# Values first in layer 0, rotary tables built a quarter wide, and the first weights on ScalarE's queue

## The chip, the core and the metric

The kernel runs on one core of a Trainium2 chip. The core has TensorE (PE: matmuls, with weight loads, PEld, beside them), VectorE (DVE), ScalarE (ACT), GpSimd (POOL), SyncE (SP, which here issues transfers) and 16 DMA engines that all queues share. The metric is device time in microseconds (us) of one execution.

## The reference, cut to what is computed

Two layers work on x, 256 tokens by 2048 channels, in f32. Each layer does:

```python
h = rms_norm(x, norm_g[l])
proj = einsum('btd,dc->btc', h, w_in[l])          # 6848 columns
rw_in, g_rw, q, k_at, v_at, g_at = split(proj)
r, k, v, xw, xa = split(bidir_token_shift(rw_in, shift_mu[l]))
y_rw = rwkv7_branch(r, k, v, xw, xa, ...)         # 16 heads, one scan per direction
qh, kh = rope(q, positions), rope(k_at, positions)
y_at = window_attention(qh, kh, v_at, sink[l])    # 16 query heads, 4 key heads, |i-j| <= 128
mix = concatenate([y_rw * silu(g_rw), y_at * silu(g_at)])
x = x + einsum('btc,cd->btd', mix, w_out[l])
```

`rope` needs the sine and cosine of position times 32 frequencies. A final rms_norm follows.

## The kernel before

Activations lie channels by tokens. The f32 products are made of a high and a low part: every weight tile of 128 x 1024 is loaded into `raw` (three buffers, SP's queue, `wload`), split by `wsplit` into `hi` (ScalarE, L239) and `lo` (VectorE, L241), two buffers each, and every 128 x 128 block of it takes three matmuls of 256 columns (L309 to L311). Such a triple is called a step here. `Stream` holds the steps of all projections in one order; `S.run(n)` issues the next n of them, and when two steps of a tile are left it issues the load and split of the next one. A layer has 864 input steps (xw and xa 32, eight head pairs of k, v, r and gate 512, attention values 32, keys 32, queries and gates 256) and 256 output steps: 2240 in all.

`window(64, ...)` runs 64 steps in 11 groups and lets generators go on between the groups: `scan_p`, `scan_i` and `scan_b` (preparation, inversion and recurrence of one head pair, one pair behind the other), `attend`, and in layer 0 `setup`, which makes constants and the rotary tables. Lists such as `ROT` and `ATT` say in which groups each goes on. TensorE's order is the program's; the other engines' instructions are placed by a scheduler with priorities, apart from those issued through `PA` and `PV`, which keep the program's order.

At the start SP's queue loads the first weight tile, norm_g, x in five parts and the second tile. ScalarE and VectorE split each of the 16 rows of x (`x_split`, L203 and L204) while TensorE, after 11 warm-up matmuls, runs one step of xw for each row. Then ScalarE squares x for the norm in four parts. Layer 0's attention values (`v_step`, L578 to L580) came in window 8; windows 0 to 9 hold scans, 10 and 11 scans and attention, 12 attention alone. The rotary tables COS and SIN are made in place, 256 tokens wide on all 128 partitions, although only 32 frequencies differ; the range reduction goes on from window 2 to window 6 and the two sine lookups are in window 7.

Of the kernel before, what the change touches and what calls it, by code (L numbers as in the profile page):

```python
# [133 lines left out]
def hybrid_trunk_kernel(ctx, tc, xT, wi, wv, wo, par, fing, dup, iup, sink, pos, cst, out):  # L134
# [207 lines left out]
    COS = cp.tile([128, T], F32, name="COS")  # L342
    SIN = cp.tile([128, T], F32, name="SIN")

    def setup():
        posi = st("t1", [T], I32, bufs=3)
        SY.dma_start(out=posi, in_=pos.to_broadcast([128, T]))
# [4 lines left out]
        for l in range(DEPTH):  # L352
            s = DP[:, l, 0:NSH]
            V.tensor_tensor(s, PR[:, l, P_MU0 : P_MU0 + NSH], PR[:, l, P_MU1 : P_MU1 + NSH], op=ALU.add)
            V.tensor_scalar(s, s, -1.0, 1.0, op0=ALU.mult, op1=ALU.add)
            h = DP[:, l, NSH : NSH + 8]
            V.tensor_scalar(h, PR[:, l, P_KA : P_KA + 8], 0.5, None, op0=ALU.mult)
            V.tensor_scalar(DP[:, l, NSH + 8 : NSH + 16], h, -1.0, 1.0, op0=ALU.mult, op1=ALU.add)
            V.tensor_scalar(DP[:, l, NSH + 16 : NSH + 32], PR[:, l, P_A0 : P_A0 + 16], 0.5, None, op0=ALU.mult)
        V.tensor_scalar(SK, SK, 8.0, None, op0=ALU.mult)  # L360
        yield

        V.tensor_copy(
# [3 lines left out]
        V.memset(MSK, 1.0)  # L367
        V.memset(MSK[:, :, 0:1], 0.0)
        V.tensor_copy(band, cin[:, 0:512])
        A.activation(BONES, ones, AF.Copy, scale=0.0)  # L370
        for r in half:
            A.activation(BONES[r, r], ones[r, r], AF.Copy)
        V.tensor_copy(EYE, cin[:, 512 + 64 * NL : 576 + 64 * NL])
        V.tensor_scalar(NEYE, EYE, -1.0, None, op0=ALU.mult)
        V.tensor_scalar(EYE2, EYE, 2.0, None, op0=ALU.mult)
# [9 lines left out]
        def reduce_by(dst, src, period, bits, shift):  # L385
            PV.tensor_scalar(nn, src, 1.0 / period, shift, op0=ALU.mult, op1=ALU.add)
            yield
            PV.tensor_scalar(nn, nn, MAGIC, MAGIC, op0=ALU.add, op1=ALU.subtract)
            yield
            cur = src  # L390
            for p in split_const(period, bits, 4):
                PV.scalar_tensor_tensor(dst, nn, -p, cur, op0=ALU.mult, op1=ALU.add)
                cur = dst
                yield

        two_pi = 2.0 * np.pi
        yield from reduce_by(ang, ang, two_pi * 4096.0, 7, 0.0)
        for dst, shift, add in ((SIN, 0.0, 0.0), (COS, 0.25, np.pi / 2)):
            yield from reduce_by(dst, ang, two_pi, 11, shift)
# [6 lines left out]
        yield  # L406
        PV.tensor_scalar(SIN, SIN, C[:, C_OFF["sgn"] : C_OFF["sgn"] + 1], None, op0=ALU.mult)
# [31 lines left out]
    def queue_inputs(l):  # L439
# [129 lines left out]
        pvs = []  # L569

        def v_step(kk, b):
            def f(w):
                if not pvs:
                    pvs.extend(ps_main.tile([128, T], F32, tag="m", name="pva") for _ in range(2))
                k = kk % 4
                wh, wl = (x[:, k * 256 : (k + 1) * 256] for x in w)
                tb = slice(b * 128, (b + 1) * 128)
                PE.matmul(pvs[b], L.XH[:, kk, tb], wh, start=(kk == 0), stop=False)  # L578
                PE.matmul(pvs[b], L.XH[:, kk, tb], wl, start=False, stop=False)
                PE.matmul(pvs[b], L.XL[:, kk, tb], wh, start=False, stop=(kk == 15))  # L580

            return f

        def v_evac():
            L.VA = st("VA", [2, 256])
            with tc.high_priority(offset=PRIO_B):
                A.activation(L.VA[:, 0, :], pvs[0], AF.Copy, scale=L.norm.rt[:, 0:1])  # L587
                V.tensor_scalar(L.VA[:, 1, :], pvs[1], L.norm.rt[:, 1:2], None, op0=ALU.mult)

        for qt in range(4):  # L590
            S.add(
                lambda qt=qt: wsplit(wload(wv[l, qt])),
                [v_step(qt * 4 + k, b) for k in range(4) for b in range(2)],
                v_evac if qt == 3 else None,
            )

        def k_place(m):
            def place():
                if m == 0:
                    L.KA = [st("KA", [2, T], F32R), [st(n, [T], F32R) for n in ("kd", "kkr")]]  # L600
                return L.KA[0][:, m, :], L.KA[1][m]

            return place
# [68 lines left out]
    def layer(l):  # L672
# [399 lines left out]
        def scores(j):  # L1072
            m, g = divmod(j, 4)
            t = L.tq[j]
            Sc = t["S"] = st("ge", [2, 2, 264], bufs=2) if j == 2 else st("mv", [2, 2, 264], bufs=3)
# [52 lines left out]
        def attend():  # L1128
# [37 lines left out]
    for k in range(NKT):  # L1166
        x_split(L0.XH, L0.XL, X0[:, k, :], k, 0)
        S.run(1)
# [9 lines left out]
    S.later(20, lambda: L0.norm.add([ACC[:, i * T : (i + 1) * T] for i in range(4)]))  # L1178
    S.later(27, lambda: L0.norm.spread())
    S.run(8)  # L1180
    SY.dma_start(out=C, in_=cst[:, 0:C_KEEP])
    SY.dma_start(out=PR, in_=par.rearrange("l p n -> p l n"))
    setup_ = setup()
    next(setup_)
    S.run(8)
    for l in range(DEPTH):
# [5 lines left out]
        if l + 1 < DEPTH:  # L1192
            S.run(32)
# [88 lines left out]
```

## Time and profile before

| | |
|---|---|
| median of 3 runs | 1171.67 us (1170.61 to 1172.37) |
| the profiled execution, its span | 1171.01 us, 1169.2 us |
| TensorE busy | 1148.4 us, 98% |
| VectorE busy | 905.4 us, 77% |
| ScalarE busy | 785.5 us, 67% |
| GpSimd busy | 21.7 us, 2% |
| moved by DMA | 166.63 MB, mean 143 GB/s |

The first row is what the prediction is held to. The profiled execution is one more run, with its own time; its span goes from the first to the last instruction shown. Busy time of TensorE is modelled, and matmuls overlap: one of 256 columns is shown as 0.28 us long while the next starts 0.12 us after it.

### The profile page before, as it was taken

What the parts mean: (1) busy time and instruction counts of PE and PEld (TensorE: products, weight loads), DVE (VectorE), ACT (ScalarE), POOL (GpSimd) and SP (SyncE); (2) the same over time, 40 slices, a digit from 0 to 9 for tenths busy, and PEclk for the clock granted to TensorE, in tenths of its full rate; (3) what the DMA queues carried; (4) which work ended last, traced back from release to release, by engine and by line L of the source; (5) the groups of instructions that cost most, each with busy time, mean ns of one, the idle gap of its engine ahead of it and who ended that gap; (6) DMA issues with size and microseconds to landing.
All of it is one profiled execution on the core that took longest, in us unless ns stands there. A gap on an engine that the chain in (4) does not pass through costs nothing.

```text
span 1169.2 us, 38101 instructions
## 1 busy us (share of the span) xinstructions
PE 1148.4 (98%) x16151; PEld 1074.6 (92%) x16151; DVE 905.4 (77%) x2012; ACT 785.5 (67%) x1986; POOL 21.7 (2%) x23
## 2 busy tenths in 40 slices
PE   8999999999999999999999999999999999999996
PEld 7988999999899999899999899999999999899996
DVE  7889978888877677766668888888887767786554
ACT  6667876787776666655556677876786666675553
POOL 0000000000000000000000000000000000000000
PEclk9999999999999999999999999999999999999998
DMA  7544334333333433477655443334333343346653
GB/s 261 168 152 134 130 106 127 97 112 113 96 116 124 134 120 121 141 238 234 212 177 176 141 135 116 106 108 131 98 112 111 121 136 122 106 144 191 213 192 127
DMA packets 60554, 166.63 MB, mean 143 GB/s; under 512 B 7744, under 2 KB 22880, under 8 KB 60384
## 3 DMA queue, kind: packets, MB, share of 16 engines
q1 hardware_dynamic: 60384, 164.21, 43.8%
q8 instruction: 126, 2.06, 0.7%
q14 instruction: 44, 0.36, 0.1%
HBM read 157.37 MB, written 4.19 MB: 138 GB/s over the span
## 4 chain that ended last, share of the span: by engine, by line
PE 75%; issue 13%; DVE 5%; ACT 4%; DMA 1%; SPq 0%; POOL 0%; POOLq 0%; DVEq 0%; ACTq 0%
PE pm L309 19%; PE pm L311 16%; PE pm L310 16%; PE pg L831 3%; PE pcc L994 2%; DVE lo L241 2%; PE pcc L1022 2%; PE pd L938 1%; PE py L1006 1%; PE py L979 1%; PE pq L929 1%; PE pcc L1012 1%; ACT hi L239 1%; DMA raw<-wi 1%; PE pza L689 1%
## 5 line engine op out<-in xcount | busy, mean ns | idle before, releaser
L241 DVE TENSOR_TENSOR lo<-raw,hi 128x512 fp32r<-128x512 f32 x560 | 372.0, 687 | 115.2 <-ACT hi L239 109.8
L239 ACT ACTIVATE hi<-raw 128x512 fp32r<-128x512 f32 x560 | 329.5, 625 | 169.7 <-PE pm L310 98.0
L309 PE MATMUL pm<-XHa,hi 128*128 128x256 f32 x832 | 245.6, 295 | 0.8 <-ACT VA L587 0.4
L309 PE MATMUL pm<-XHb,hi 128*128 128x256 f32 x832 | 243.5, 293 | 0.2
L311 PE MATMUL pm<-XHb,lo 128*128 128x256 f32 x832 | 234.2, 281 | 1.4 <-DVE lo L241 1.4
L311 PE MATMUL pm<-XHa,lo 128*128 128x256 f32 x832 | 234.1, 281 | 1.2 <-DVE lo L241 1.0
L310 PE MATMUL pm<-XLb,hi 128*128 128x256 f32 x832 | 234.0, 281 | 0.4 <-DVE XLb L204 0.4
L310 PE MATMUL pm<-XLa,hi 128*128 128x256 f32 x832 | 234.2, 281 | 0.1
L309 PEld LDWEIGHTS pm<-XHa,hi 128*128 128x128 f32 x832 | 157.1, 189 | 11.4 <-ACT XHa L203 1.3
L309 PEld LDWEIGHTS pm<-XHb,hi 128*128 128x128 f32 x832 | 157.0, 189 | 6.0 <-ACT hi L239 0.3
L311 PEld LDWEIGHTS pm<-XHa,lo 128*128 128x128 f32 x832 | 157.2, 189 | 2.5 <-DVE lo L241 2.4
L311 PEld LDWEIGHTS pm<-XHb,lo 128*128 128x128 f32 x832 | 157.2, 189 | 2.1 <-DVE lo L241 2.0
L310 PEld LDWEIGHTS pm<-XLa,hi 128*128 128x128 f32 x832 | 157.4, 189 | 0.7 <-DVE XLa L204 0.7
L310 PEld LDWEIGHTS pm<-XLb,hi 128*128 128x128 f32 x832 | 157.3, 189 | 0.6 <-DVE XLb L204 0.6
L1017 ACT ACTIVATE suv<-pcc 64x128 f32<-64x128 f32 x128 | 34.5, 270 | 72.3 <-PE pcc L1015 48.4
L309 PE MATMUL pm<-MHa,hi 128*128 128x256 f32 x256 | 72.0, 281 | 0.0
L311 PE MATMUL pm<-MHb,lo 128*128 128x256 f32 x256 | 71.8, 280 | 0.0
L310 PE MATMUL pm<-MLa,hi 128*128 128x256 f32 x256 | 71.8, 280 | 0.0
L310 PE MATMUL pm<-MLb,hi 128*128 128x256 f32 x256 | 71.7, 280 | 0.0
L309 PE MATMUL pm<-MHb,hi 128*128 128x256 f32 x256 | 71.7, 280 | 0.0
L311 PE MATMUL pm<-MHa,lo 128*128 128x256 f32 x256 | 71.7, 280 | 0.0
L309 PEld LDWEIGHTS pm<-MHa,hi 128*128 128x128 f32 x256 | 48.2, 188 | 0.8 <-issue 0.8
(291 smaller groups left out, 2322.7 us busy)
## 6 DMA issues: line engine op xcount, KB each, us to landing
raw<-wi SPq DMA_DIRECT2D x207, 512.0 KB
raw<-wo SPq DMA_DIRECT2D x64, 512.0 KB
raw<-wv SPq DMA_DIRECT2D x8, 512.0 KB
rrot<-u SPq DMA_DIRECT2D x80, 32.0 KB
vg<-xT SPq DMA_DIRECT2D x16, 128.0 KB
xd<-vg SPq DMA_DIRECT2D x16, 128.0 KB
vg<-xd SPq DMA_DIRECT2D x16, 128.0 KB
g<-dup SPq DMA_DIRECT2D x16, 97.0 KB
```

The source lines that it names most:

```text
L239: A.activation(hi[:, q], raw[:, q], AF.Copy)
L241: V.tensor_tensor(lo[:, q], raw[:, q], hi[:, q].bitcast(F32), op=ALU.subtract)
L309: PE.matmul(pm, wh, rh[:, kk, :], start=(kk == 0), stop=False)
L310: PE.matmul(pm, wh, rl[:, kk, :], start=False, stop=False)
L311: PE.matmul(pm, wl, rh[:, kk, :], start=False, stop=(kk == 15))
L689: PE.matmul(o, w[0], x[0], start=True, stop=False)
L831: PE.matmul(pg[:, h, c * 128 : (c + 1) * 128], BK[half[h], d, c, 1 - h : 3 - h, :].rearrange("p s j -> p (s j)"), MV[half[h], d, c].rearra ...
L929: PE.matmul(narrow(pq[:, d], h ^ d, c), hq(AB, d, c, h), sub(TC, h, d, c, d * b), start=True, stop=True)
L938: PE.matmul(narrow(pd[:, d], h, c), hx(TT, d, c, h), sub(QF, h ^ d, d, c, d * b), start=True, stop=True)
L994: PE.matmul(pc[half[h], 0, d, :], GE[h][r, d, ci[d], 0, :], SUV[r, d, ci[d], h, :], start=True, stop=True)
L1017: A.activation(here(h), pc[half[h], 1], AF.Copy)
L1022: PE.matmul(pS[half[h], d, :], BT[:, h, d, i, :], SUV[:, d, ci[d], h, :], start=(i == 0), stop=True, skip_group_check=True)
```

## The change

Layer 0 now runs its 32 value steps first: each row of x serves two steps (one for each half of the tokens) instead of one, and 32 steps are run while x is split. xw and xa follow, in the two banks of one pair. The windows begin after 64 steps instead of 32. Layer 1 runs its values right after xw and xa, and S.run(64) stands between the layers. Window 12 has 32 steps; the attention begins one window earlier, relative to the scans, and its calls are spread by a new `ATT`. The setup is issued in program order (`PV`, `PA`), spread by a new `ROT` over windows 0 to 4. The rotary angles are laid out as 4 quarters of 64 tokens on 4 groups of 32 partitions, so that each operation is 64 columns wide; sixteen transfers on SP's queue spread the result. The first weights and norm_g are issued by ScalarE. The transfers of C and PR are issued within the loop over x.

```diff
 ATT = [
-    [3, 9],
-    [1, 3, 5, 6, 8, 10],
-    [0, 2, 4, 5, 6, 8, 9, 10],
+    [9],
+    [1, 4, 8],
+    [0, 2, 3, 5, 6, 8, 9],
+    [0, 1, 2, 3, 4],
 ]
-ROT = {0: [2, 3], 1: [], 7: [2, 5, 7], 8: [1, 3], 9: []}
+ROT = ([2, 4, 6, 9], [2, 7], [0, 3, 5, 8], [2, 6], [5])
...
-    first_w = [wrp.tile([128, 1024], F32, tag="raw", name="raw") for _ in range(2)]
+    first_w = [wrp.tile([128, 1024], F32, tag="raw", name="raw") for _ in range(3)]
...
-    SY.dma_start(out=first_w[0][:, 0:512], in_=wi[0, 0, 0, :, 0:512])
-    SY.dma_start(out=G0, in_=par[0, :, P_NG : P_NG + NKT])
+    A.dma_start(out=first_w[0][:, 0:512], in_=wv[0, 0, :, 0:512])
+    A.dma_start(out=G0, in_=par[0, :, P_NG : P_NG + NKT])
     for a, b in ((0, 2), (2, 4), (4, 8), (8, 12), (12, 16)):
         SY.dma_start(out=X0[:, a:b, :], in_=xT[:, a:b, :])
         if a == 0:
-            SY.dma_start(out=first_w[0][:, 512:1024], in_=wi[0, 0, 0, :, 512:1024])
-        if a == 4:
-            SY.dma_start(out=first_w[1], in_=wi[0, 0, 1])
+            SY.dma_start(out=first_w[0][:, 512:1024], in_=wv[0, 0, :, 512:1024])
+        if a in (2, 4):
+            SY.dma_start(out=first_w[a // 2], in_=wv[0, a // 2])
...
-    COS = cp.tile([128, T], F32, name="COS")
-    SIN = cp.tile([128, T], F32, name="SIN")
+    TRIG = cp.tile([128, 2, T], F32, name="TRIG")
+    SIN, COS = TRIG[:, 0], TRIG[:, 1]
     def setup():
-        posi = st("t1", [T], I32, bufs=3)
-        SY.dma_start(out=posi, in_=pos.to_broadcast([128, T]))
+        posi = st("t1", [64], I32, bufs=3)
+        quarter = [slice(i * 32, (i + 1) * 32) for i in range(4)]
+        for i, q in enumerate(quarter):
+            SY.dma_start(out=posi[q], in_=pos[:, i * 64 : (i + 1) * 64].to_broadcast([32, 64]))
...
-        AN = st("VA", [2, T])
-        ang, nn = AN[:, 0], AN[:, 1]
-        V.tensor_copy(ang, posi)
-        yield
+        AN = st("KA", [4, 64])
+        ang, nn, table = AN[:, 0], AN[:, 1], AN[:, 2:4]
+        PV.tensor_copy(ang, posi)
...
-        for dst in (SIN, COS):
-            PA.activation(dst, dst, AF.Sin)
+        PA.activation(table, table, AF.Sin)
         yield
+        PV.tensor_copy(band, cin[:, 0:512])
+        yield
+        for i, q in enumerate(quarter):
+            for r in quarter:
+                SY.dma_start(out=TRIG[r, :, i * 64 : (i + 1) * 64], in_=table[q])
+            yield
         PV.tensor_scalar(SIN, SIN, C[:, C_OFF["sgn"] : C_OFF["sgn"] + 1], None, op0=ALU.mult)
...
+        turns = [(k, b) for k in range(4) for b in range(2)] if l == 0 else [(k, b) for b in range(2) for k in range(4)]
+        done = (lambda: S.later(23, v_evac)) if l == 0 else v_evac
...
         if l == 0:
-            inproj(0, lambda pm: S.later(29, lambda: xw_evac(pm)), raws=first_w, bank=lambda: wbank("pm")[:, 0:T])
-            inproj(1, lambda pm: S.later(13, lambda: xa_evac(pm)))
+            values_in()
...
+        if l == 0:
+            inproj(0, lambda pm: S.later(13, lambda: xw_evac(pm)), bank=lead_bank(0))
+            inproj(1, lambda pm: S.later(4, lambda: xa_evac(pm)), bank=lead_bank(1))
         else:
             inproj(0, xw_evac)
             inproj(1, xa_evac)
+            values_in()
...
-                if j < 6:
+                if 0 < j < 6:
                     scores(j + 2)
                 yield
                 if j < 7:
                     flip(j + 1)
+                    if j == 0:
+                        scores(2)
                     yield
-        for w in range(NP + 2):
-            window(64, *scans(w), *([(setup_, ROT.get(w, [2, 5, 9, 9]))] if l == 0 else []))
+        for w in range(NP + 1):
+            window(64, *scans(w), *([(setup_, ROT[w])] if l == 0 and w < len(ROT) else []))
         att = attend()
-        window(64, *scans(NP + 2), (att, ATT[0]))
-        window(64, *scans(NP + 3), (att, ATT[1]))
-        window(64, (att, ATT[2]))
+        for i in range(3):
+            window(64, *scans(NP + 1 + i), (att, ATT[i]))
+        window(32, (att, ATT[3]), groups=len(ATT[3]))
...
         x_split(L0.XH, L0.XL, X0[:, k, :], k, 0)
-        S.run(1)
+        S.run(2)
+        if k == 11:
+            SY.dma_start(out=C, in_=cst[:, 0:C_KEEP])
+            SY.dma_start(out=PR, in_=par.rearrange("l p n -> p l n"))
...
-    S.later(20, lambda: L0.norm.add([ACC[:, i * T : (i + 1) * T] for i in range(4)]))
-    S.later(27, lambda: L0.norm.spread())
+    S.later(18, lambda: L0.norm.add([ACC[:, i * T : (i + 1) * T] for i in range(4)]))
+    S.later(25, lambda: L0.norm.spread())
+    setup_ = setup()
     S.run(8)
-    SY.dma_start(out=C, in_=cst[:, 0:C_KEEP])
-    SY.dma_start(out=PR, in_=par.rearrange("l p n -> p l n"))
-    setup_ = setup()
     next(setup_)
-    S.run(8)
+    S.run(24)
...
         if l + 1 < DEPTH:
-            S.run(32)
+            S.run(64)
```

## Rows read from the trace of the kernel before

**Rows 1.** The page's busy times: engine, us (share of the span), instructions.

```profile
PE 1148.4 (98%) x16151; PEld 1074.6 (92%) x16151; DVE 905.4 (77%) x2012; ACT 785.5 (67%) x1986; POOL 21.7 (2%) x23
```

**Rows 2.** Timeline of the start: start, us, what, idle before it and its releaser.

```profile
1.22 4.88 PE L1162 MATMUL warm<-QF 128*128 128x512 f16 x11 [1.22 <-DVE QF L1157]
...
1.64 0.43 SPq L325 DMA_DIRECT2D X0a<-xT  x1
...
5.95 0.51 ACT L203 ACTIVATE XHa<-X0a,G 128x256 fp32r<-128x256 f32 x1 [2.00 <-DMA X0a<-xT]
...
6.51 0.58 PE L309 MATMUL pm<-XHa,hi 128*128 128x256 f32 x1 [0.42 <-ACT XHa L203]
...
9.63 0.41 PE L309 MATMUL pm<-XHa,hi 128*128 128x256 f32 x1
...
10.27 0.41 PE L309 MATMUL pm<-XHa,hi 128*128 128x256 f32 x1
...
11.16 0.28 PE L309 MATMUL pm<-XHa,hi 128*128 128x256 f32 x1
...
11.48 3.29 ACT L203 ACTIVATE XHb<-X0b,G 128x256 fp32r<-128x256 f32 x8
11.51 0.28 PE L309 MATMUL pm<-XHa,hi 128*128 128x256 f32 x1
...
15.72 1.99 ACT L254 ACTIVATE mv<-X0a 128x1024 f32<-128x1024 f32 x2
```

**Rows 3.** TensorE's groups by line from 6.40 to 37.15 us: count, busy, mean, idle before.

```profile
L309 PE MATMUL pm<-XHa,hi 128*128 128x256 f32 x32 | 10.1, 314 | 0.4 <-ACT XHa L203 0.4
...
L311 PE MATMUL pm<-XHb,lo 128*128 128x256 f32 x32 | 9.1, 284 | 1.2 <-DVE lo L241 1.2
L216 PE MATMUL pr<-C,mv 128*128 128x1 f32 x16 | 1.8, 245 | 0.0
L224 PE MATMUL pr<-C,rt 128*128 128x128 f32 x4 | 0.6, 274 | 0.0
```

**Rows 4.** The page's costliest groups: the splits of the weights.

```profile
L241 DVE TENSOR_TENSOR lo<-raw,hi 128x512 fp32r<-128x512 f32 x560 | 372.0, 687 | 115.2 <-ACT hi L239 109.8
L239 ACT ACTIVATE hi<-raw 128x512 fp32r<-128x512 f32 x560 | 329.5, 625 | 169.7 <-PE pm L310 98.0
```

**Rows 5.** Windows: span, busy of PE, PEld, DVE, ACT, POOL; granted clock; DMA.

```profile
50.20:78.92 28.72, 27.23 (x242) 26.15 (x240) 26.70 (x51) 20.27 (x45) 0.00 (x0) 1.00 0.50 160
...
189.69:230.53 40.84, 40.29 (x753) 37.25 (x751) 34.97 (x76) 30.52 (x82) 1.31 (x1) 1.00 0.36 110
270.63:313.92 43.29, 41.48 (x753) 38.47 (x751) 35.52 (x75) 33.91 (x86) 1.31 (x1) 0.96 0.33 104
...
764.03:803.89 39.86, 39.86 (x753) 37.03 (x751) 34.01 (x72) 30.41 (x82) 1.31 (x1) 1.00 0.34 113
843.86:883.72 39.86, 39.86 (x753) 37.02 (x751) 34.69 (x74) 30.40 (x82) 1.31 (x1) 1.00 0.36 113
```

**Rows 6.** Timelines of ScalarE and of TensorE near 293 us, in window 7.

```profile
292.80 1.28 ACT L254 ACT_TABLE_LOAD   x1
...
295.54 0.30 PE L938 MATMUL pd<-QF,tt 64*64 64x32 f16 x16 [1.81 <-ACT tt L900]
```

**Rows 7.** The stretch after that wait, columns as in Rows 5.

```profile
297.40:300.80 3.40, 3.40 (x28) 3.18 (x31) 3.13 (x9) 2.88 (x9) 0.00 (x0) 0.50 0.00 0
```

**Rows 8.** The tile VA, VectorE: operations of the range reduction, min/median/max ns.

```profile
L254 DVE SCALAR_TENSOR_TENSOR VA<-VA x4: 416/416/416, 108.1 to 142.9; 128x256 f32<-128x256 f32 x4
```

**Rows 9.** Waits of TensorE and of SP's queue: us in total, times, longest.

```profile
PE pbn L704 <- DVE ip L254: 2.2, 2, 1.1
...
SPq L552 <- ACT u L550: 14.0, 4, 5.4
```

**Rows 10.** Timeline of window 12: last scores, end of their softmax.

```profile
481.26 0.39 PE L1085 MATMUL pscr<-KA,kr 64*128 64x256 f32 x2
...
486.92 0.61 DVE L1103 TENSOR_SCALAR mv<-mv,den 128x256 f32<-128x256 f32 x2
```

More of the change, by code (lines that the diff above doesn't have):

```diff
@@ L353, in setup @@
             s = DP[:, l, 0:NSH]
-            V.tensor_tensor(s, PR[:, l, P_MU0 : P_MU0 + NSH], PR[:, l, P_MU1 : P_MU1 + NSH], op=ALU.add)
-            V.tensor_scalar(s, s, -1.0, 1.0, op0=ALU.mult, op1=ALU.add)
+            PV.tensor_tensor(s, PR[:, l, P_MU0 : P_MU0 + NSH], PR[:, l, P_MU1 : P_MU1 + NSH], op=ALU.add)
+            PV.tensor_scalar(s, s, -1.0, 1.0, op0=ALU.mult, op1=ALU.add)
             h = DP[:, l, NSH : NSH + 8]
[L357 to L360, printed above, removed]
-        yield
-        V.tensor_copy(
+            PV.tensor_scalar(h, PR[:, l, P_KA : P_KA + 8], 0.5, None, op0=ALU.mult)
+            PV.tensor_scalar(DP[:, l, NSH + 8 : NSH + 16], h, -1.0, 1.0, op0=ALU.mult, op1=ALU.add)
+            PV.tensor_scalar(DP[:, l, NSH + 16 : NSH + 32], PR[:, l, P_A0 : P_A0 + 16], 0.5, None, op0=ALU.mult)
+        PV.tensor_scalar(SK, SK, 8.0, None, op0=ALU.mult)
+        V.memset(MSK, 1.0)
+        V.memset(MSK[:, :, 0:1], 0.0)
+        yield
+        PA.activation(BONES, ones, AF.Copy, scale=0.0)
+        for r in half:
+            PA.activation(BONES[r, r], ones[r, r], AF.Copy)
+        PV.tensor_copy(EYE, cin[:, 512 + 64 * NL : 576 + 64 * NL])
+        PV.tensor_scalar(NEYE, EYE, -1.0, None, op0=ALU.mult)
+        PV.tensor_scalar(EYE2, EYE, 2.0, None, op0=ALU.mult)
+        yield
+        PV.tensor_copy(
             LV.rearrange("p l s (n x) -> p (l s) n x", x=32),
@@ L393, in reduce_by @@
                 cur = dst
-                yield
         two_pi = 2.0 * np.pi
-        yield from reduce_by(ang, ang, two_pi * 4096.0, 7, 0.0)
-        for dst, shift, add in ((SIN, 0.0, 0.0), (COS, 0.25, np.pi / 2)):
-            yield from reduce_by(dst, ang, two_pi, 11, shift)
+        reduce_by(ang, ang, two_pi * 4096.0, 7, 0.0)
+        yield
+        for i, (shift, add) in enumerate(((0.0, 0.0), (0.25, np.pi / 2))):
+            dst = table[:, i]
+            reduce_by(dst, ang, two_pi, 11, shift)
             if add:
@@ L494, in split, with v_step, f, v_evac @@
             V.tensor_tensor(lo, x[0:rows], hi.bitcast(F32), op=ALU.subtract)
-        if l == 0:
-            inproj(0, lambda pm: S.later(29, lambda: xw_evac(pm)), raws=first_w, bank=lambda: wbank("pm")[:, 0:T])
-            inproj(1, lambda pm: S.later(13, lambda: xa_evac(pm)))
+        pvs = []
+        def v_step(kk, b):
+            def f(w):
+                if not pvs:
+                    pvs.extend(ps_main.tile([128, T], F32, tag="m", name="pva") for _ in range(2))
+                k = kk % 4
+                wh, wl = (x[:, k * 256 : (k + 1) * 256] for x in w)
+                tb = slice(b * 128, (b + 1) * 128)
+                PE.matmul(pvs[b], L.XH[:, kk, tb], wh, start=(kk == 0), stop=False)
+                PE.matmul(pvs[b], L.XH[:, kk, tb], wl, start=False, stop=False)
+                PE.matmul(pvs[b], L.XL[:, kk, tb], wh, start=False, stop=(kk == 15))
+            return f
+        def v_evac():
+            L.VA = st("VA", [2, 256])
+            with tc.high_priority(offset=PRIO_B):
+                A.activation(L.VA[:, 0, :], pvs[0], AF.Copy, scale=L.norm.rt[:, 0:1])
+                V.tensor_scalar(L.VA[:, 1, :], pvs[1], L.norm.rt[:, 1:2], None, op0=ALU.mult)
+        turns = [(k, b) for k in range(4) for b in range(2)] if l == 0 else [(k, b) for b in range(2) for k in range(4)]
+        done = (lambda: S.later(23, v_evac)) if l == 0 else v_evac
+        raws = first_w if l == 0 else []
+        def values_in():
+            for qt in range(4):
+                S.add(
+                    lambda qt=qt: wsplit(raws[qt] if qt < len(raws) else wload(wv[l, qt])),
+                    [v_step(qt * 4 + k, b) for k, b in turns],
+                    done if qt == 3 else None,
+                )
+        if l == 0:
+            values_in()
+        lead = []
+        def lead_bank(i):
+            def bank():
+                if not lead:
+                    lead.append(wpair("pm"))
+                return lead[0][:, i, 0:T]
+            return bank
+        if l == 0:
+            inproj(0, lambda pm: S.later(13, lambda: xw_evac(pm)), bank=lead_bank(0))
+            inproj(1, lambda pm: S.later(4, lambda: xa_evac(pm)), bank=lead_bank(1))
         else:
@@ L567, in rope_evac @@
             return evac
[L569 to L595, printed above, removed]
         def k_place(m):
```

18 lines of the change are left out of this document (5 added, 13 removed).

## Prediction

> **What bounds the kernel now.** I read the busy times first: TensorE is busy for 98% of the span [rows 1], and its order is the program's. The change keeps every matmul, so it can only take out time in which TensorE waits or runs slowly. The second view is therefore the start. TensorE's first useful matmul comes at 6.51 us, 0.42 us after the warm-up and released by the first split row of x [rows 2]. Up to 37.15 us it makes 64 steps, 32 in each half of the rows, and the norm's 20 small matmuls [rows 3]. At full pace a step takes 0.35 us (11.16 to 11.51), early on 0.64 us (9.63 to 10.27) [rows 2]; 256 columns in 0.21 us are the lower of the two clock levels, 1.2 GHz, and that pace lasted to about 10.6 us. So the floor is 64 x 0.35 + 1.8 + 0.6 = 24.8 us [rows 2, 3], the elapsed time 37.15 - 6.51 = 30.6 us, and 5.8 us are lost: to the low clock, to rows of x that ScalarE and VectorE hand over one by one, and 1.2 us to a late low part of a weight tile [rows 3], after the squares of x had held ScalarE (1.99 us for two of four) [rows 2].
>
> The third view compares the windows of the two layers, which run the same instructions but for the setup in layer 0. The stretches shown are windows 1, 5 and 7 of layer 0 and windows 5 and 7 of layer 1 [rows 5]. Window 5 takes 40.84 us against 39.86, window 7 takes 43.29 against 39.86. In window 7 the chain is plain: ScalarE switches its table for the sines, 1.28 us, and TensorE waits 1.81 us for a small inversion tile tt that stands behind it [rows 6]; then the granted clock is 0.50, the lower level, for 3.4 us, with 28 matmuls in it [rows 7].
>
> **The start.** Values first gives two steps for each split row of x. The warm-up ends at 1.22 + 4.88 = 6.10 us [rows 2]. x now is first on SP's queue, where it stood behind two issues and was issued at 1.64, so the split row should be there by then; 6.51 - 6.10 = 0.4 us come from this. The two issues on ScalarE's queue cost it 2 x 0.43 us, by SP's row, ahead of its first table load, long before it needs x at 5.95 [rows 2]: nothing. If the cover failed, the 0.4 us would be lost again and no more. I keep the low clock to 10.6 us: 4.5 us make 7.0 steps instead of 12.9, so 5.9 x 0.35 = 2.1 us are lost. The squares still come between two weight tiles, so I keep that 1.2 us. For rows of x that come late I add 0.5 us: ScalarE needs 3.29 us for eight rows, 0.41 each [rows 2], against 0.70 us for two steps, but it has four more half tiles to split before the last row. Lost then 3.8 us instead of 5.8, and the 64 steps end at 6.1 + 24.8 + 3.8 = 34.7 instead of 37.15: 2.4 us gained. Bounds: if those four half tiles at 0.625 us [rows 4] all lie on the path, 2.5 us are given back and nothing is gained; if only the low clock costs, 37.15 - 33.0 = 4.1. I take 2.4, because ScalarE's rate for rows leaves room for most of the splits. The 32 steps that are put ahead are missing later in window 8, so the rest of the program is as long as before.
>
> **The old setup in windows 2 to 7.** It leaves windows 5 and 7. Their excess over layer 1 goes with it: 40.84 - 39.86 = 1.0 and 43.29 - 39.86 = 3.4, together 4.4 us [rows 5]. The excess could in part be layer 0's own for another reason, but TensorE's wait in window 7 names its releaser, so I take all of it; the lower end is 3.4 for window 7 alone.
>
> **The new setup.** The sines now stand at the start of window 2: one activation of 128 columns, a switch there and one back, 2 x 1.28 + about 0.3 = 2.9 us of ScalarE (the 0.3 is an estimate from 0.51 us for 256 columns) [rows 2, 6]. What is late next are the exponentials of scan_p and the high parts of the weights. ScalarE waits for TensorE to free those buffers, 98.0 us in all [rows 4], so it usually runs ahead; and the first inversion has only just begun there, so no tt is due. Price between 0 and the 3.4 us that the old one cost; I take 1.0, nearer to nothing, as the deadline that was missed is not there.
>
> VectorE: 24 operations of the range reduction and its ends become 64 columns wide. The row of 256 columns is 0.416 us [rows 8]; 64 lie between a quarter of that, 0.10, and all of it, and I estimate 0.2. Fifteen of them are now in window 1, which had none, and where VectorE is already busy 26.70 of 28.72 us [rows 5], with TensorE waiting for it at the bonus sums (2.2 us in two waits, one in each layer) [rows 9]. 15 x 0.2 = 3.0 us make 29.7, which is 1.0 us more than the window holds. Price between 0 and 3.0; I take 1.0. The constants that window 0 gets (their operations stood at the start before) lie beside 32 more steps without scans ahead of it: nothing; without that cover they would be part of the same 3.0.
>
> SP's queue: sixteen transfers of the tables and three more of the positions, by 0.43 us an issue [rows 2], 8.2 us in all, four at a time, 1.7 us, before the next weight load. The first stand behind the sines on ScalarE, and weight loads stand behind them. Such a wait is ordinary here: the rotation of the queries waits on ScalarE on the same queue, 14.0 us in all, 5.4 at the longest [rows 9], and TensorE is busy all the while. So nothing; without that cover 4 x 1.7 = 6.9 us. C and parameters move ahead of SP's other setup loads, and GpSimd gets nothing new.
>
> **Attention.** Window 12 has 32 steps instead of 64 in both layers. The last head's scores begin at 481.26, its softmax ends at 486.92 + 0.61, so the chain is 6.3 us [rows 10]. From its scores to its transposes there were four groups of 5.8 steps, 8.1 us; now there are three of 6.4, 6.7 us, and the other heads' matmuls beside. That is enough: nothing, at worst 0.5 us in each layer.
>
> **Sum.** 1171.0 (the profiled execution's own time) - 2.4 - 4.4 + 1.0 + 1.0 = 1166.2. That execution was 0.66 us under the median of the runs, so against the median I say 1166.9.
>
> **The Trainium skill on the table switch.** The page "ScalarE: Activation LUTs", section "What ACT_TABLE_LOAD costs", counts a drain of about 1.38 us on top of the 1.28 us load, 2.66 us for each switch. This trace does not show that drain: from the load's start at 292.80 to TensorE's restart at 295.54 are 2.74 us, and two sines and two copies lie in there besides. By the page the two switches would hold ScalarE some 5.6 us, and the time would be that of the first rival.
>
> **Rivals.** *The table switch takes its stall along.* In window 2 the exponentials come one group after the sines, so both switches follow close on each other while VectorE is nearly full; if TensorE starves and its clock falls as in window 7, the price is 3.4 instead of 1.0, and the time 1169.3. For it speaks the old stall, against it that no inversion result is due yet. Chance 0.15.
>
> *ScalarE bounds the start.* The rows, eight half tiles and four squares are one queue; if it paces TensorE all through, the waits only change their names, the 2.4 us stay, and the time is 1169.3: this part then does not do what it is made for. For it speaks the 1.2 us wait for a low part, against it that ScalarE waited 2.00 us for x before its first row. Chance 0.12. Both together, 1171.7: 0.04.
>
> *The shorter last window starves TensorE; slower than before.* The chain of 6.3 us has 6.7 us of steps over it. When weight splits and gates lengthen the chain beyond that, each of the last three transposes waits. To end over 0.2% slower it must cost 4.8 + 2.3 = 7.1 us, 3.6 in each layer, or 1.2 us for each of three heads: about 1174. Against it speaks that softmax work ran between weight splits in this row's chain already. Chance 0.06.
>
> **The numbers.** The forecast has the remaining 0.63. Its own range is 1163.2 (4.1 at the start, both new prices nothing) to 1169. The range for 8 in 10 reaches over the first two rivals and half a price more: 1162.8 to 1170.5. A measurement can tell some 0.2%, 2.3 us, from no change. Faster than that are the forecast and half of each of the first two rivals, 0.77; within it the other halves and both together, 0.17; slower the last rival, 0.06.
>
> **What would show it.** Right: the 64th step ends near 34.7 us, with the squares' wait still there; windows 5 and 7 of layer 0 take 39.9 us like layer 1's; no stretch of granted clock 0.50 near 293 us. Wrong: a wait over 1 us right after the table switch in window 2 with a low clock behind it; window 1 longer than 30 us with waits on VectorE; TensorE waiting for P or for the transposes in window 12; weight loads that land late behind the table transfers.

## The result, and the profile after

The changed kernel takes 1176.14 us (median of 6 runs, 1174.23 to 1179.03), the kernel before 1171.14 us (6 runs, 1170.18 to 1172.37): ratio 1.0042, interval 1.0030 to 1.0054. It is 5 us slower where 4.8 us less were forecast, and outside the range. The profiled execution of the changed kernel is the slowest of its six, 1179.03 us, so the ledger below, made from the two profiled executions, ends at +8.0 us and not at +5.0.

The page's busy times, beside [rows 1], say that the work is what it was: TensorE has 0.7 us more, VectorE and ScalarE have a little less.

```profile
PE 1149.1 (98%) x16151; PEld 1076.1 (91%) x16151; DVE 903.1 (77%) x2012; ACT 783.9 (67%) x1985; POOL 21.7 (2%) x23
```

So the 8 us are time in which TensorE waits or runs at the lower clock, and the place is found by windows. The view of windows of the changed kernel has the columns of [rows 5]; the first five lines are windows 1, 2, 5 and 7 of layer 0 and window 1 of layer 1, the last two are stretches within windows 1 and 2.

```profile
59.08:95.54 36.46, 29.87 (x243) 28.80 (x241) 28.28 (x65) 20.64 (x46) 0.00 (x0) 0.86 0.41 129
95.54:134.81 39.27, 34.52 (x465) 31.89 (x463) 29.93 (x59) 27.35 (x60) 0.00 (x0) 0.96 0.39 121
212.75:252.61 39.86, 39.86 (x753) 37.03 (x751) 34.02 (x72) 30.40 (x82) 1.31 (x1) 1.00 0.36 113
292.58:332.44 39.86, 39.86 (x753) 37.02 (x751) 34.70 (x74) 30.41 (x82) 1.31 (x1) 1.00 0.36 112
643.83:672.30 28.47, 27.19 (x243) 26.11 (x241) 26.36 (x50) 20.30 (x45) 0.00 (x0) 1.00 0.50 162
...
81.54:91.78 10.24, 5.98 (x28) 5.98 (x29) 5.93 (x16) 2.04 (x4) 0.00 (x0) 0.50 0.23 83
119.09:122.50 3.41, 3.41 (x30) 3.36 (x31) 3.41 (x9) 3.35 (x12) 0.00 (x0) 0.50 0.14 26
```

The ledger. Up to window 7 a window holds the same steps in both traces; its length goes from the start of its first step to the start of the next window:

| stretch | before, us | after, us | change |
|---|---|---|---|
| 64 steps end | 37.21 | 34.81 | -2.4 |
| window 1 | 28.72 | 36.46 | +7.7 |
| window 2 | 33.62 | 39.27 | +5.7 |
| window 4 | 40.11 | 40.88 | +0.8 |
| window 5 | 40.84 | 39.86 | -1.0 |
| window 7 | 43.28 | 39.86 | -3.4 |
| layer 1, first step to last | 568.55 | 568.88 | +0.3 |

What is left (windows 0 and 8 to 12 with the 32 steps that moved set apart, windows 3 and 6, layer 0's output, the end) is under 0.5 us each. The start and windows 5 and 7 gave back the 6.8 us that were forecast. But window 4 now takes 40.88 us against 40.0 in layer 1, so 0.8 us of this stand one window earlier. That excess goes with the place of the setup's last operation: in e5 and e6, where it is in window 5, that window takes 40.9 and 40.8 us and window 4 39.9 and 40.0; in e3, where it is in group 8 of window 4 instead of group 5, no window has it. Windows 1 and 2 took 13.4 us. In both, TensorE waits and the granted clock is 0.50, 1.2 GHz, for 10.24 us in window 1 (from 2 us into the wait) and for 3.41 us in window 2 (from the end of the wait). Of the 10.24 us, 5.98 have matmuls in them; they start 0.21 us apart there and 0.12 us apart at the granted clock of 1.00, so the loss is some 5.98 x (1 - 0.12 / 0.21) = 2.6 us, and 1.5 us in window 2. The view of TensorE's waits names what it waited for (us in total, times, longest), beside [rows 9], where the first of them was 2.2 us with 1.1 as the longest:

```profile
PE pbn L728 <- DVE ip L255: 7.3, 2, 6.2
PE pd L962 <- ACT tt L924: 4.7, 3, 4.0
```

**Window 1.** pbn is the sum of the bonus, two matmuls on the high and the low part of the tile ip. The timeline has the wait, and ScalarE's high part 7 us ahead of it, done in time:

```profile
78.36 0.42 ACT L255 ACTIVATE ip<-th 128x256 fp32r<-128x256 f32 x1 [0.22 <-DVE th L255]
...
85.80 0.58 PE L728 MATMUL pbn<-ip,BONES 128*128 128x256 f32 x1 [6.24 <-DVE ip L255]
```

The low part is VectorE's. Its timeline between the two (start, us):

```profile
80.12 0.18 DVE L255 TENSOR_SCALAR KA<-KA 128x64 f32<-128x64 f32 x1
80.22 0.68 DVE L242 TENSOR_TENSOR lo<-raw,hi 128x512 fp32r<-128x512 f32 x1
80.83 0.18 DVE L255 TENSOR_SCALAR KA<-KA 128x64 f32<-128x64 f32 x1
...
82.00 0.21 DVE L255 SCALAR_TENSOR_TENSOR KA<-KA 128x64 f32<-128x64 f32 x1
82.13 1.74 DVE L255 RECIPROCAL kd<-kd 128x256 f32<-128x256 f32 x1
83.80 0.16 DVE L255 SCALAR_TENSOR_TENSOR KA<-KA 128x64 f32<-128x64 f32 x1
...
84.79 0.18 DVE L255 TENSOR_SCALAR KA<-KA 128x64 f32<-128x64 f32 x1
...
85.23 0.18 DVE L255 TENSOR_SCALAR KA<-KA 128x64 f32<-128x64 f32 x1
85.33 0.42 DVE L255 TENSOR_TENSOR ip<-th,ip 128x256 fp32r<-128x256 f32 x1
```

KA is the tile of the range reduction. Its eight operations for the cosine come from group 7 of the window, each behind the one before, 1.5 us of work; the low part comes from group 8. VectorE ran all eight first, and in the gaps between them weight splits, gate work and a reciprocal of 1.74 us. From 80.12 us on these 1.5 us of work, and what ran in their gaps, kept a 0.42 us operation waiting until 85.33, whose input had been there since 78.8. The lines L255 are those issued through `PV` and `PA`, of which I said ahead of the prediction that they keep the program's order. That does not hold throughout: the reciprocal is issued through `PV` too, for the next head pair and from group 2 of window 2, well behind the low part, and yet it ran ahead of it. In the kernel before it ran behind the low part (72.0 to 71.3 us). What the mark does to the scheduler's order beyond that, the traces don't show.

**Window 2.** tt, the inversion's small tile, is ScalarE's. ScalarE's timeline, the table switches first:

```profile
95.95 1.28 ACT L255 ACT_TABLE_LOAD   x1
97.25 0.31 ACT L255 ACTIVATE KA<-KA 128x128 f32<-128x128 f32 x1
97.58 1.28 ACT L255 ACT_TABLE_LOAD   x1
...
116.95 1.15 ACT L240 ACTIVATE hi<-raw 128x512 fp32r<-128x512 f32 x2 [6.66 <-DMA raw<-wi]
...
118.67 0.37 ACT L924 ACTIVATE tt<-pq 128x256 f16<-128x256 f32 x1
```

The switches are over at 98.86 us. The loss comes 18 us later: the high part of a weight tile waits 6.66 us for its load, tt stands behind it, and TensorE waits 4.02 us for tt. The issues on SP's queue show why that load is late (first the queue's wait, then its issues in order of time):

```profile
SPq L411 <- ACT hi L240: 5.0, 1, 5.0
```

```profile
97.31 0.32 SPq L562 DMA_DIRECT2D g<-dup  x1
97.67 13.24 SPq L411 DMA_DIRECT2D TRIG<-KA  x13
111.01 1.00 SPq L232 DMA_DIRECT2D raw<-wi  x2
112.06 1.87 SPq L411 DMA_DIRECT2D TRIG<-KA  x3
```

Thirteen of the sixteen table transfers went in one row. The first stood 5.0 us for ScalarE, the 13 then took about 0.6 us each, and the weights came after them. The sines were done at 97.56 us, and the table was ready by then: in e1 below, on GpSimd's queue, the first transfer goes at 97.85.

```profile
97.85 2.30 POOL L411 DMA_DIRECT2D TRIG<-KA  x4 [68.20 <-ACT KA L255]
```

What held the row on SP's queue beyond that, the trace doesn't show. The name of the releaser is inferred; the row went when that high part was done, at 102.6 us.

### The profile page after: what moved, and what is told of

Same layout as the page of the kernel before. It is cut to its first block, busy times and chain, and to the rows that moved or that the text cites. A ratio compares the mean times of both kernels' runs of the same rounds, so it can differ in the third digit from the quotient of the medians.

```text
span 1177.2 us, 38117 instructions
## 1 busy us (share of the span) xinstructions
PE 1149.1 (98%) x16151; PEld 1076.1 (91%) x16151; DVE 903.1 (77%) x2012; ACT 783.9 (67%) x1985; POOL 21.7 (2%) x23
## 4 chain that ended last, share of the span: by engine, by line
PE 74%; issue 12%; DVE 6%; ACT 3%; DMA 3%; SPq 0%; POOL 0%; DVEq 0%; POOLq 0%; ACTq 0%
PE pm L310 19%; PE pm L312 16%; PE pm L311 16%; PE pg L855 3%; DVE lo L242 2%; PE pcc L1018 2%; DMA raw<-wi 2%; PE pd L962 1%; PE pcc L1046 1%; PE py L1003 1%; PE py L1030 1%; PE pq L953 1%; PE pcc L1036 1%; ACT hi L240 1%; PE pscr L1109 1%
```

## The experiments

All are edits of the changed kernel, timed in 5 rounds beside the kernel before on the same chip. They ran in three batches on three chips, where the kernel before has medians of 1171.99, 1171.79 and 1171.59 us; between batches the ratio to it says more than a difference of medians. Lengths of windows are those of each one's profiled execution. Windows without a loss are taken from layer 1 of the changed kernel: 28.5 us for window 1, 33.4 us for window 2.

### SP's queue in window 2

**e1_tables_on_gpsimd** gives the sixteen transfers to GpSimd's queue, on which no weights stand; e12 below has the counter-test.

```diff
-                SY.dma_start(out=TRIG[r, :, i * 64 : (i + 1) * 64], in_=table[q])
+                G.dma_start(out=TRIG[r, :, i * 64 : (i + 1) * 64], in_=table[q])
```

> The sixteen table transfers are issued by GpSimd instead of SyncE; all else is as changed. If the loss in window 2 comes from weight loads queued behind thirteen transfers of 0.6 us on SyncE, the window falls from 39.3 to about 33.5 us, no wait over 1 us for tt is left there, window 1 stays at 36.5, and the median falls from 1176.1 by 4 to 6 us to about 1171. If the two table switches on ScalarE cause it, window 2 stays near 39 us and the median near 1176.

1172.23 us (before 1171.99; ratio 1.0005, interval 0.9996 to 1.0014). Its windows 1 and 2:

```profile
59.28:95.50 36.22, 29.60 (x242) 28.52 (x240) 28.26 (x65) 20.63 (x45) 0.00 (x0) 0.91 0.40 131
95.50:129.73 34.23, 33.26 (x464) 30.50 (x462) 29.85 (x59) 27.69 (x60) 8.62 (x16) 1.00 0.44 138
```

Window 2 falls from 39.27 to 34.23 us with both table switches still in it, window 1 stays. So the queue costs 5.0 us between these two executions (that of the changed kernel is its slowest) and 3.9 us between the medians, and what the switches can cost is the rest over layer 1, at most 0.8 us.

### Window 1: the order or the amount of work

**e2_setup_unordered** takes the mark for program order from the range reduction.

```diff
-            PV.tensor_scalar(nn, src, 1.0 / period, shift, op0=ALU.mult, op1=ALU.add)
+            V.tensor_scalar(nn, src, 1.0 / period, shift, op0=ALU.mult, op1=ALU.add)
...
-                PV.scalar_tensor_tensor(dst, nn, -p, cur, op0=ALU.mult, op1=ALU.add)
+                V.scalar_tensor_tensor(dst, nn, -p, cur, op0=ALU.mult, op1=ALU.add)
```

> The range reduction is issued without the program-order mark; the operations and their groups are the same. If the order is what makes the bonus's low part late (it must stand behind eight dependent operations and what fills the gaps between them), the wait for ip in window 1 falls from 6.2 to 1 to 2 us, the low clock behind it goes, window 1 takes 29 to 30 us instead of 36.5, and the median falls by 5 to 7 us to about 1170. If the added work is what does it, VectorE has as much to do as before, window 1 stays over 34 us and the median over 1174. Window 2 stays near 39 us either way.

1168.36 us (ratio 0.9970, interval 0.9959 to 0.9980). Window 1:

```profile
59.21:88.24 29.03, 27.34 (x243) 26.25 (x241) 26.62 (x51) 20.29 (x45) 0.00 (x0) 1.00 0.51 166
```

The loss is gone. Window 2, expected to stay near 39 us, falls to 36.65. But VectorE has 51 instructions in window 1 here and not 65, 26.62 us and not 28.28: without the mark the scheduler placed the whole reduction between 51.3 and 59.4 us, in window 0, so work left the window too, and this run alone doesn't separate the two.

**e9_bonus_unmarked** leaves the reduction where it is and takes the mark from the low part instead and gives it a high priority (that of the inversion's casts).

```diff
-            low(bonus, km[:, 0:T])
+            with tc.high_priority(offset=PRIO_TC):
+                V.tensor_tensor(bonus[:, 1], km[:, 0:T], bonus[:, 0].bitcast(F32), op=ALU.subtract)
```

> As changed, with the one low part of the bonus sums taken out of the marked order and given priority, in all windows of both layers; the range reduction stays where it is. If its place in the queue is what made it late, not the work around it, the wait for ip in window 1 falls from 6.2 us to under 0.5, no low clock follows, and window 1 takes 28.5 to 30 us instead of 36.5; layer 1's window 1 may gain some 1 us too, as its wait of 1.1 us goes. Window 2 stays near 37 to 39 us (the transfers). Median 1168 to 1170.5. If the added work is the matter, TensorE waits elsewhere in window 1, which stays over 33 us, and the median over 1173.

1172.21 us (ratio 1.0008, interval 1.0000 to 1.0017). Window 1, and one line of TensorE's waits:

```profile
58.99:87.15 28.16, 27.33 (x242) 26.23 (x241) 26.75 (x62) 20.41 (x45) 0.00 (x0) 1.00 0.50 167
```

```profile
PE pm L312 <- DVE lo L242: 8.6, 15, 0.8
```

The window has its chain (62 instructions on VectorE, 49 in window 1 of its layer 1) and is at full pace, and no wait for ip is left. Beside window 1 of its own layer 1, 27.3 us, the chain costs 0.9 us: that is the work. The rest of the 8 us was the order: the low part runs at 79.31 us, the eight operations from 80.85 to 85.35 us, behind it. The median missed its expectation, for the edit holds in every window of both layers, and in most of them TensorE now waits some 0.6 us for a low part of the weights, about 2 us behind the bonus: 8.6 us in 15 waits, where the changed kernel has 1.3 in 5 for that line; windows 5 to 7 take 40.8 us each instead of 39.9.

Five runs move the chain by the setup's list; two of them, e6 and e10, move the transfers to GpSimd's queue as well. In the changed kernel that list is `([2, 4, 6, 9], [2, 7], [0, 3, 5, 8], [2, 6], [5])`, a list of groups for each of windows 0 to 4; the sine's reduction is in group 2 of window 1, the cosine's in group 7.

**e3_cosine_in_window_2** lets the cosine's reduction go on in group 0 of window 2, behind the bonus of window 1, and all that follows one place later.

```diff
-ROT = ([2, 4, 6, 9], [2, 7], [0, 3, 5, 8], [2, 6], [5])
+ROT = ([2, 4, 6, 9], [2], [0, 3, 5, 8], [2, 6], [5, 8])
```

> The cosine's range reduction goes on in group 0 of window 2 instead of group 7 of window 1, everything behind it one entry later. Both theories of window 1 expect its wait to fall to about 1.5 us and the window to 29 to 30 us. If order is the matter, the same chain may now hold up a low part in window 2 instead; the table transfers come later, so SyncE's block moves to windows 3 and 4 and costs up to 4 us there. Median 1168 to 1173; not under 1167 as long as the transfers stand in a row.

1165.76 us (1164.72 to 1165.89; ratio 0.9948, interval 0.9935 to 0.9960), better than expected. Window 1 takes 29.8 us, window 2 34.7, although the transfers stayed on SP's queue. Its issues:

```profile
101.21 6.19 SPq L411 DMA_DIRECT2D TRIG<-KA  x8
...
108.08 3.15 SPq L411 DMA_DIRECT2D TRIG<-KA  x5
...
111.90 2.77 SPq L411 DMA_DIRECT2D TRIG<-KA  x3
```

The same sixteen went in rows of 8, 5 and 3 with weight loads between them, and the first stood 1.2 us instead of 5.0. The rows are the scheduler's; why the new list gives other ones, the trace doesn't show.

**e5_window_1_free** puts both reductions into window 2 (`[2, 4, 6, 9], [], [2, 7], [0, 3, 5, 8], ...`), **e6_window_1_free_gpsimd** does so with the transfers on GpSimd's queue.

> Window 1 holds no setup; sine, cosine and lookup go on in windows 2 and 3; thirteen table transfers stand in a row on SyncE's queue again, now in window 3. Window 1 should take 28.7 us as in layer 1. If the row of transfers is what cost window 2 its 5 us, window 3 loses 3 to 6 us now (40 to 43 instead of 37.05), and the median is 1168 to 1171. If the loss needs the crowded VectorE of window 2, window 3 stays under 38.5 us and the median under 1167.

> As e5, with the table transfers on GpSimd's queue. Both causes are then gone: window 1 28.7, window 2 33.5 to 34.5, window 3 37.0 to 38, no low clock before the end, and the median 1164 to 1165.5, under e3's 1165.8. If something else of the new setup costs (the table switch or the chain in program order), windows 2 and 3 keep over 2 us and the median stays over 1166.

1171.28 us (ratio 0.9995, interval 0.9985 to 1.0006) and 1170.21 us (0.9984, 0.9973 to 0.9995); both missed. Window 1 is free (28.9 and 28.9 us), but window 2 has its own bonus, and the chain in group 7 now stands ahead of that one. In e5 the wait for ip is

```profile
PE pbn L728 <- DVE ip L255: 5.2, 3, 3.1
```

with a granted clock of 0.50 for 6.8 us behind it, and window 2 takes 39.1 us; in e6 a wait of 3.1 us, 3.4 us of low clock, and 37.8 us. What counts isn't the window but whether the chain stands ahead of a bonus. The row of 13 transfers in e5, one window later and without its long stand, cost 0.8 us (window 3: 37.9 to e6's 37.1).

**e10_reduction_in_window_0** takes both reductions into window 0, where only the first pair's preparation begins (`[1, 2, 4, 5, 7, 9], [], [0, 3, 5, 8], ...`), transfers on GpSimd's queue; **e12_reduction_in_window_0_synce** is the same with SP's queue.

> The whole range reduction goes on in window 0, where VectorE has room, window 1 holds no setup, the lookup stands at the start of window 2 as in the changed kernel and the table transfers are on GpSimd's queue. Both causes are gone if they are the two that were named: window 0 24.4 to 25, window 1 28.7, window 2 33.4 to 34.3, windows 5 and 7 39.9, no low clock before the end; median 1163.5 to 1165.5, under e3. If the table switch costs by itself, window 2 stays over 35 us and the median over 1166.

> As e10 with the transfers on SyncE, thirteen in a row in window 2. e5 showed 0.8 us for such a row in window 3 when the first transfer did not wait, so the price should be set by how long the first one stands for ScalarE: with a stand of 4 to 5 us, window 2 takes 36 to 39 us and the median 1166.5 to 1170; without it, 34 to 35 us and 1164.5 to 1166.

1165.94 us (1165.02 to 1168.43; ratio 0.9954, interval 0.9942 to 0.9966) and 1168.51 us (0.9973, 0.9963 to 0.9982). In e10 window 0 takes 24.26 us as in the changed kernel, so the reduction costs nothing there, and windows 1 and 2 are clean:

```profile
59.04:87.91 28.87, 27.24 (x242) 26.17 (x241) 26.44 (x50) 20.28 (x45) 0.00 (x0) 1.00 0.54 171
87.91:122.12 34.21, 33.26 (x465) 30.50 (x463) 29.83 (x59) 27.71 (x60) 8.62 (x16) 1.00 0.45 139
```

In e12 window 2 takes 36.4 us: 13 transfers in one row again, and a stand of 4.4 us.

```profile
91.40 11.89 SPq L411 DMA_DIRECT2D TRIG<-KA  x13
```

The queue's price with a row of 13 is thus 0.8 us (e5, no long stand), 2.2 us (e12 against e10), 2.5 us (e2 against e11 below) and 5.0 us (the changed kernel against e1). The number of issues alone doesn't set it, nor does the stand: it is 4.4, 4.3 and 5.0 us in the last three. In e12, e2, e7 and the changed kernel the row ends 14.4, 14.9, 15.1 and 15.4 us after the first step of window 2; TensorE's longest wait for tt there is 1.1, 1.4, 1.9 and 4.0 us, and the window takes 36.4, 36.7, 37.2 and 39.3 us, with 3.4 us of low clock in the last two. Why the last us costs so much more isn't shown.

### The low clock behind a wait

**e7_wait_filled** puts 28 matmuls of zeros, 512 columns each, into pbn's bank just ahead of the bonus sums of window 1. It adds work and leaves nothing out.

```diff
+            if l == 0 and p == 0:
+                for _ in range(28):
+                    PE.matmul(pb, zeros[:, 0:128], zeros, start=True, stop=True)
```

> 28 matmuls of zeros, 512 columns each (some 0.21 us), are put ahead of the bonus sums of the first head pair, into the bank that these overwrite; they fill the 6.2 us wait of window 1 with work and change nothing else. If the low clock behind that wait is a cost of its own, the window falls from 36.5 to 31 to 32 us with no stretch of 0.50 in it and the median by 3 to 5 us, though TensorE gets work added. If the low clock costs nothing that the wait does not hide, the window stays at 36 to 37 us and the median at 1176.

1172.64 us (ratio 1.0002, interval 0.9993 to 1.0011), 3.5 us under the changed kernel. Window 1:

```profile
59.26:92.89 33.63, 33.30 (x271) 28.89 (x269) 28.31 (x65) 20.57 (x45) 0.00 (x0) 1.00 0.44 141
```

VectorE's chain is as long as it was, the granted clock stays at 1.00 in this window. The window was expected at 31 to 32 us and takes 33.6: the filled wait still costs 5, the low clock with the empty one cost 36.46 - 33.63 = 2.8 us more, near the 2.6 worked out above. So this wait of TensorE had two prices. The median says less of it, as window 2 is 2.1 us shorter here too (37.2 us).

### The start

**e8_first_weights_on_synce** is e3 with the first weights and norm_g on SP's queue again, ahead of x.

```diff
-    A.dma_start(out=first_w[0][:, 0:512], in_=wv[0, 0, :, 0:512])
-    A.dma_start(out=G0, in_=par[0, :, P_NG : P_NG + NKT])
+    SY.dma_start(out=first_w[0][:, 0:512], in_=wv[0, 0, :, 0:512])
+    SY.dma_start(out=G0, in_=par[0, :, P_NG : P_NG + NKT])
```

> As e3, but the first half tile of weights and norm_g are issued by SyncE again. By the prediction the queue is worth at most the 0.4 us between the warm-up and the first split row: the 64th step ends at 34.7 to 35.2 us and the median is that of e3, 1165.8, to 1166.3. If two queues bring the first rows of x clearly sooner, step 64 ends over 1 us later and the median is over 1166.8.

1166.98 us (1165.97 to 1168.36) to e3's 1165.76. The 64th step ends at 36.06 us, in e3 at 34.69. The splits of rows 4 to 7 of x, e8 first, then e3:

```profile
10.72 1.71 ACT L204 ACTIVATE XHa<-X0a,G 128x256 fp32r<-128x256 f32 x4 [0.82 <-DMA X0a<-xT]
```

```profile
9.39 1.71 ACT L204 ACTIVATE XHa<-X0a,G 128x256 fp32r<-128x256 f32 x4
```

So with the first weights on ScalarE's queue the later rows come 1.3 us sooner. The medians differ by 1.2 us, but the two ran in different batches, and their ratios, 0.9954 (0.9940 to 0.9969) and 0.9948 (0.9935 to 0.9960), can't be told apart; e8 also has 3.4 us of low clock in window 1, which takes 31.1 us there. The 64th step is the better witness: in the eleven profiled executions with the new start, the new setup and two queues it ends between 34.66 and 35.05 us.

**e4_old_setup** keeps the new order of the steps and brings back the old setup: its constants without marks, tables in place over 256 tokens, its old list.

> The new start, order of values and attention with the old setup: wide tables in place, no transfers, the old groups. If the new start is worth 2.4 us by itself, window 1 takes 28.7 and window 2 33.6 us as before the change, window 7 may again lose some 3 us at the sines, and the median is about 1168.7 (1167 to 1170). If the new start is what pushes work into windows 1 and 2, they stay over 32 and 36 us and the median stays at 1174 or more.

1172.72 us (ratio 1.0013, interval 1.0003 to 1.0022), a miss. Windows 1 and 2 take 28.8 and 33.6 us as expected, so the new start isn't what loads them. The old setup's loss is back: window 5 takes 40.9 us, window 7 43.3. But the start lost its gain too, the 64th step ends at 39.20 us. VectorE's timeline:

```profile
31.64 0.96 DVE L364 CAST LV<-mv 128x1536 uint8<-128x1536 f32 x1 [5.04 <-DMA mv<-cst]
```

The unmarked cast of a constant was placed early, and its operand's transfer was late; VectorE stood 5.04 us, TensorE 1.9 us for a low part, then 3.4 us of low clock followed. In the changed kernel the cast is marked and comes later in the program; it ran at 43.54 us, in window 0, without a wait.

### Both repairs

**e11_unordered_gpsimd** is e2 and e1 together.

> e2's unmarked range reduction and e1's transfers on GpSimd together. If the two losses are separate, they add: window 1 29.0 as in e2, window 2 33.5 to 34.3 as in e1, median 1165 to 1166.5, 2 to 3 us under e2. If they are one (the late chain of window 1 delaying window 2), window 2 falls no further than e2's 36.65 and the median stays near 1168.

1165.69 us (1164.05 to 1166.00; ratio 0.9945, interval 0.9933 to 0.9957). Windows 1 and 2:

```profile
59.06:87.92 28.86, 27.25 (x242) 26.18 (x241) 26.64 (x51) 20.27 (x45) 0.00 (x0) 1.00 0.51 167
87.92:122.08 34.16, 33.18 (x464) 30.44 (x462) 29.82 (x59) 27.68 (x60) 8.62 (x16) 1.00 0.46 139
```

Against the changed kernel's median e2 gains 7.8 us, e1 3.9, both 10.5 (by the ratios 0.7, 0.4 and 1.0%): two losses that nearly add. They aren't quite separate, as e2 alone took 2.6 us from window 2. This version, e3 and e10 can't be told apart, and all three beat both kernels.

## Why the prediction failed, point by point

**The start: right in its sum, not in its make-up.** Forecast 34.7 us for the 64th step, measured 34.81. The first matmul is at 5.77 us, 0.3 us under what I took, and the stretch is 29.0 - 24.8 = 4.2 us over my floor, where I had 3.8; but the terms are others. I kept the low clock to 10.6 us as in [rows 2], 2.1 us; TensorE's timeline after has

```profile
5.77 0.58 PE L511 MATMUL pva<-hi,XHa 128*128 128x256 f32 x1
6.50 0.39 PE L513 MATMUL pva<-hi,XLa 128*128 128x256 f32 x1
6.72 0.28 PE L511 MATMUL pva<-hi,XHa 128*128 128x256 f32 x1
6.84 0.28 PE L512 MATMUL pva<-lo,XHa 128*128 128x256 f32 x1
...
32.43 0.28 PE L312 MATMUL pm<-XHb,lo 128*128 128x256 f32 x1
33.30 0.39 PE L310 MATMUL pm<-XHb,hi 128*128 128x256 f32 x1 [0.59 <-DVE u L457]
```

matmuls 0.12 us apart from 6.7 us on, so 0.6 us were lost there and not 2.1. And where the low clock lasted, it was hardly worth anything: e12 has the same start, and in its execution the matmuls are 0.21 us apart until 10.3 us,

```profile
10.09 0.41 PE L511 MATMUL pva<-hi,XHa 128*128 128x256 f32 x1
10.30 0.33 PE L512 MATMUL pva<-lo,XHa 128*128 128x256 f32 x1
```

yet its 64th step ends at 35.05 us, 0.2 us later, without the waits for split rows of x that TensorE has here. So at the lower clock TensorE only came later to rows that it otherwise waits for; in this my second rival was right, and the 2.4 us came all the same. The waits must be read from start to start: 32.43 to 33.30 is 0.87 us where 0.12 would do, 0.75 us lost with an idle time of 0.59, and the matmul after it comes 0.1 us late too. So read, 1.2 us go to split rows of x (I had 0.5), 1.3 to two late low parts of weight tiles (I had 1.2), 0.9 to the reader of the xw sums (not in my sum) and 0.2 to the steps behind the norm's matmuls; with the 0.6 these are the 4.2. The sum came out right by errors that cancel, which is luck. I said that without the cover of ScalarE's queue 0.4 us would be lost and no more: e8 loses 1.4 us, at rows 4 to 7, which my bound left out. The Trainium skill, "DMA: Bandwidth & Descriptors", section "Issuing engines are not separate DMA queues", grants a second issuing engine the issue time alone. Two issues of 0.43 us [rows 2] are 0.9 us, and in e8 the load of rows 4 to 7 is issued 0.9 us later than in e3 (3.55 to 2.63 us), but the rows came 1.3 us later; the rest isn't explained, and it is one execution of each.

**The old setup's places: 3.6 of the 4.4 us.** Windows 5 and 7 take 39.86 us each, 4.4 us less, and e4 brings the loss back with the setup. But window 4 took 0.8 us more, so the excess of 1.0 us that I took off window 5 went to the place of the new setup's last operation, and the lower end, 3.4 for window 7 alone, was nearer.

**The table switch: right, at most 0.8 us for the 1.0 forecast.** My rival put its 3.4 us stall into this window, and a stall with a low clock did come there, but e1 removes it and leaves the switches: the rival's mechanism was wrong. The Trainium skill, "ScalarE: Activation LUTs", section "What ACT_TABLE_LOAD costs", adds a drain of about 1.38 us to every switch. This trace shows none: the sines start 0.02 us behind their load's end (95.95 + 1.28 to 97.25), the second load starts 0.02 us behind the sines, and it ends at 98.86 us.

**The step that failed first: the price of VectorE's work in window 1, "Price between 0 and 3.0; I take 1.0".** The durations were right (0.16 to 0.22 us for 64 columns, estimate 0.2), the amount too. I priced an amount of work, as if it were spread over the window, and held it against VectorE's free time. It is a chain of dependent operations that ran ahead of a deadline: the low part of the bonus, for which [rows 9] already showed VectorE 1.1 us late. By e9 the same work behind the low part costs 0.9 us in that window, so the 1.0 was right for what it priced. In its place stood 7.7 us, of which some 2.8 are the low clock (e7). The step named the bonus sums, but priced the engine's load alone: not how long the low part would stand behind the added operations and what fills their gaps, nor the low clock after a wait, though [rows 7] shows one. Two of the signs of being wrong that I listed are what came: window 1 over 30 us with a wait on VectorE, and weight loads that land late behind the table transfers.

**The step that failed second: "So nothing; without that cover 4 x 1.7 = 6.9 us".** I took the sixteen transfers as four groups with weight loads between, by the order in the source, and an issue as 0.43 us. The queue's order is the scheduler's: 13 in one row, 0.6 us each, behind a stand of 5.0 us. The bound without cover, 6.9 us, was nearer: 5.0 us by e1, 2.2 to 2.5 by e12 and e2. I took the lower end because the rotation's wait, up to 5.4 us [rows 9], hurt nothing; there four transfers go in a row ahead of the weights, here 13 did, 8 us of them. The time of an issue stood in the trace that I had, in such a row without a wait (0.6 us each):

```profile
363.30 2.42 SPq L552 DMA_DIRECT2D rrot<-u  x4
```

**Attention: right.** Windows 8 to 12 cost 0.2 us less in layer 0 and 0.8 less in layer 1, with the 32 steps at 0.35 us set apart; the rival of the short last window did not come.

With the two failed terms put right, the sum holds. The recorded terms without the two new prices give 1171.1 - 2.4 - 4.4 = 1164.3 us, and e11, which has neither of the two stalls, measures 1165.7 (by its ratio 1164.7). In its profiled execution windows 1, 2 and 4 are 0.1, 0.5 and 0.7 us longer than in the kernel before, which makes up the 1.4. What stays open is why the scheduler forms a row of 13 in one kernel and of 8, 5 and 3 in another, and why it put the reciprocal ahead of the low part: I saw its result alone. What held the first transfer for 5.0 us stays open too, and why the same row costs 2.2 us in one kernel and 5.0 in another; the low clock's part of window 2, some 1.5 us, is worked out and not measured by itself.

## What to carry to other kernels

An operation added to an engine is priced by what stands behind it: look for the next deadline on that engine, and ask whether the operation, its dependent chain and whatever fills the chain's gaps can stand ahead of it; free time in the window says nothing on that. On a queue of transfers count the longest row that the scheduler could form and the wait of its first, and put transfers that wait for an engine on a queue that carries nothing urgent. To a wait of TensorE add the low clock that may follow it: here 6.2 us of waiting came with 2.8 us more.

## What the runs showed of the hardware

Apart from the end of each run, the granted clock of 0.50 came in stretches with a wait of TensorE before or at their start: 3.4 us with a wait of 1.1 (e12, layer 1), 1.9 (e4, e7), 2.2 (e8), 3.1 (e6) and 4.0 us (the changed kernel); 6.8 us with one of 3.1 (e5) and of 6.2 (e1); 10.24 us with one of 6.2 (the changed kernel). The wait alone gives neither the length nor whether the clock falls: the same wait for ip of 2.2 us had no low clock behind it in e3, that of 1.1 us none in e10. In e7, with the place of the 6.2 us filled with matmuls, there was none either. Transfers of a table quarter, on-chip to on-chip, took SP's queue about 0.6 us an issue (3.15 us for 5, 6.19 for 8 with waits in it), where the loads took 0.32 to 0.50 us.
